# Weight halves interleaved word by word, moving tiles read from the last word down

## The chip, the core and the metric

The kernel runs on one core of a Trainium2 chip. The metric is the device time of one execution in microseconds (us). Five engines work side by side, each on its own queue of instructions: TensorE (PE in the profile; its weight loads are shown as PEld), VectorE (DVE), ScalarE (ACT), GpSimd (POOL) and SyncE (SP, which here only issues DMAs). Operands lie in SBUF, 128 partitions wide; matmul results lie in PSUM. An instruction that needs another engine's result waits on a semaphore.

A matmul has two operands. The stationary one (the weights, here 128 x 128) is loaded into the array by a weight load of its own; the moving one (here 128 x 256 or 128 x 512) is then streamed through. The weight load of the next matmul runs beside the streaming of the current one.

## The reference

One decoder layer on 512 tokens with a model width of 1024, all in float32:

```python
x = x + 0.5 * swiglu(rms_norm(x, g_ffn1), w_ffn1_gate, w_ffn1_up, w_ffn1_down)
proj = rms_norm(x, g_mix) @ w_in                 # 1024 x 1536
y_attn = sliding_window_attention(...)           # 8 heads, window 128, rotary, sinks
y_conv = conformer_conv(...)                     # 31 taps, LayerNorm, swish
y_mem  = memory_cross_attention(...)             # 4 heads, 256 memory tokens
x = x + concatenate([y_attn, y_conv, y_mem]) @ w_out
x = x + 0.5 * swiglu(rms_norm(x, g_ffn2), w_ffn2_gate, w_ffn2_up, w_ffn2_down)
```

with `swiglu(x, g, u, d) = (silu(x @ g) * (x @ u)) @ d` and a hidden width of 2816. Nearly all of the arithmetic is in the two SwiGLU blocks.

## The kernel before

**Precision by three products.** Every large product is made of float32r matmuls. Each operand is split into a high half (a copy cast to float32r) and a low half (the value less its high half). A product is then high x high, high x low and low x high, added up in PSUM. `mm3` (L339) issues these three for each block of 128 rows of the contraction: L347 and L348 both take the high weights `wh`, with the high and the low moving tile; L349 takes the low weights `wl` with the high moving tile. `product` (L439) does the same in L444 to L446.

**Weights.** The class `Weights` (L86) is a queue. Each item is a tile of 128 x 1024 float32 that a DMA brings from memory (`load_to`, L132), three loads ahead. `split_to` (L145) runs three items ahead of use: ScalarE writes the high half (L167), VectorE the low half (L168). The two halves are two tiles of 1056 words, `whi` and `wlo`, in four slots each; the half starts in its tile at a distance that `off` chooses (L159 to L162). With a tile of 4224 bytes both halves of an item begin at the same distance past a multiple of 256 bytes: 0 where `off` is 0, 128 where it is 128. A third kind of item, `vhi` and `vlo` (512 columns, L154), comes from the weights of the up product. The first two items are split in pieces by hand (`load_piece`, `split_piece`, L174 to L180), so that the first matmuls can start early.

**Moving tiles.** The activations' halves are tiles of 128 x 512 from `atile` (L291): `xh`, `xl` (the scaled input), `hh`, `hl` (the hidden layer), `yh`, `yl` (the outputs of the three head groups, some of them from the pool `mix`, L757) and `mh`, `ml` (the memory tokens). ScalarE writes the high one, VectorE the low one (for example L358 and L359, L402 and L403). Two small tiles named `shift` (L287, L430) only move what is allocated behind them by 128 and 64 bytes.

**The feed-forward blocks.** `ffn` (L394) runs over 22 blocks of 128 hidden columns. The first four are direct: gate and up, 8 x 3 matmuls with 512 moving columns each. From the fifth on, `fast` (L448) makes gate and up of a block together as a 2 x 2 block product in Strassen's way, with seven products of 256 moving columns (7 x 4 x 3 matmuls) in place of eight. Their moving tiles `bh` and `bl` (L427) are made once by `blocks`; the sums of weights that they need come from `make_sums` (L120). The down product runs in six rounds (`ROUNDS`, L77) between these blocks (`down`, L484). In the first round its matmuls have 512 moving columns, later on two times 256.

**The middle.** `mixing` (L747) projects the input (`proj`, 12 weight items, 512 moving columns) and runs convolution, windowed attention and memory attention in an order written out by hand (`ORDER`, L65). The attention products, transposes and sums are plain float32 matmuls (for example L826, L877, L948, L962). The output product goes through `mm3` again. The memory tokens are projected inside the first feed-forward block (`memory`, L580); for the values (L646 to L648) the roles are swapped, so that `mh` and `ml` are the weights of TensorE and the weight tile is the moving one.

Of the kernel before, what the change touches and what calls it, by code (L numbers as in the profile page):

```python
# [31 lines left out]
F32R = mybir.dt.float32r  # L32
# [6 lines left out]
P = 128  # L39
T = 512  # L40
KT = 8
# [37 lines left out]
N_ACT = 20  # L79
# [6 lines left out]
class Weights:  # L86
# [5 lines left out]
    def __init__(self, nc, pool, dma_ahead, conv_ahead, bufs):  # L92
        self.nc, self.pool = nc, pool
        self.dma_ahead, self.conv_ahead, self.bufs = dma_ahead, conv_ahead, bufs
        self.loads, self.items = [], []
        self.raw, self.after, self.split, self.piece = {}, {}, {}, {}
        self.sums = {}
        self.extra = None
        self.by_hand = 2
        self.loaded = self.done = self.at = self.turn = 0  # L100

    def add(self, ap, off=0):

        self.loads.append(ap)
        i = len(self.loads) - 1
        self.items.append((i, int(np.prod(ap.shape[1:])), off, lambda: self.raw[i]))

    def add_pair(self, gate, up, mid):
# [36 lines left out]
    def split_to(self, n):  # L145
        nc = self.nc
        while self.done < min(n, len(self.items)):
            i = self.done
            need, cols, off, src = self.items[i]
            self.load_to(need + 1)  # L150
            if need in self.after:
                self.after.pop(need)()
            if off is None:
                hi, lo = (self.extra.tile([P, cols], F32R, tag=t, name=f"{t}{i}", bufs=1) for t in ("vhi", "vlo"))  # L154
            else:

                j = self.turn % self.bufs[1]
                self.turn += 1
                hi, lo = (  # L159
                    self.pool.tile([P, 1024 + 32], F32R, tag=f"{t}{j}", name=f"{t}{i}", bufs=1)[:, c : c + 1024]  # L160
                    for t, c in (("whi", off // 4), ("wlo", 32 - off // 4))
                )  # L162
            if i < self.by_hand:
                self.piece[i] = (src(), hi, lo)
            else:
                raw = src()
                nc.scalar.copy(hi[:, :cols], raw[:, :cols])  # L167
                nc.vector.tensor_tensor(lo[:, :cols], raw[:, :cols], hi[:, :cols].bitcast(F32), op=ALU.subtract)  # L168
            self.split[i] = (hi, lo)
            self.done += 1  # L170
            if i >= self.by_hand:
                self.load_to(need + 1 + self.dma_ahead)
# [16 lines left out]
def per_load(r):  # L189

    return 8 // (ROUNDS[r][1] - ROUNDS[r][0])


def steps(f):

    r = next(r for r, (lo, hi) in enumerate(ROUNDS) if lo <= f < hi)
    if r == 0:
        return [], [], []
    m = KT // per_load(0)
    if r == 1:  # L200
        i = f - ROUNDS[1][0]
        return [(0, g) for g in range(m - 1)] if i == 0 else [], [(0, m - 1)] if i == 1 else [], []

    queue = [(q, g) for q in range(1, len(ROUNDS) - 1) for g in range(KT // per_load(q))]
    return [], [queue[f - ROUNDS[2][0]]], []


def layer(tc, ctx, a):
# [10 lines left out]
    def nm(s):  # L219
        uid[0] += 1  # L220
        return f"{s}_{uid[0]}"
# [10 lines left out]
    def work():  # L232
        return tmp.tile([P, T], F32, tag="t", name=nm("t"), bufs=5)
# [5 lines left out]
    W = Weights(nc, wpool, dma_ahead=3, conv_ahead=3, bufs=(4, 4))  # L239

    def flat(w):
        return w.rearrange("p k m -> p (k m)")

    def ffn_weights(n, memory):
        gu = a[f"wgu{n}"]

        def down(r, g):
            lo, hi = ROUNDS[r]
            m = per_load(r)
            return a[f"wd{n}"][g * m : (g + 1) * m, :, lo:hi].rearrange("d p k m -> p d (k m)")  # L250

        for f in range(NF):
            pre, mid, post = steps(f)
            for d in pre:
                W.add(down(*d), 128)
            if f < N_DIRECT:
                W.add(flat(gu[f, 0]))
                W.add(flat(gu[f, 1]))
            else:
                W.add_pair(flat(gu[f, 0]), flat(gu[f, 1]), [down(*d) for d in mid])  # L260
            for d in post:
                W.add(down(*d), 128)
            if memory and f == MEM_F:
                for t in range(2):
                    W.add(flat(a["wmk"][t]), 128)
                for c in range(2):
                    W.add(flat(a["wmv"][:, 4 * c : 4 * c + 4]))
        r = len(ROUNDS) - 1
        for g in range(KT // per_load(r)):
            W.add(down(r, g), 128)  # L270

    ffn_weights(1, True)
    for t in range(12):
        W.add(flat(a["win"][t]))
# [4 lines left out]
    for d in range(6, KT):  # L279
        W.add(flat(a["wout_z"][d - 6]))  # L280
    ffn_weights(2, False)


# [4 lines left out]
    act = ctx.enter_context(tc.tile_pool(name="act", bufs=1))  # L288
    xh, xl = {}, {}

    def atile(name, dtype=F32R):  # L291
        return act.tile([P, T], dtype, tag="h", name=nm(name), bufs=N_ACT)

    nc.scalar.dma_start(par, a["par"])
    warm = tmp.tile([P, T], BF16, tag="t", name="warm", bufs=5)
# [98 lines left out]
    def ffn(pool, norm, first, gain, hooks, next_gain, last):  # L394
# [3 lines left out]
        bh, bl = {}, {}  # L398
# [18 lines left out]
        def blocks(k):  # L417

            raw = pool.tile([P, 4, 256], F32, tag="sum", name=nm("braw"), bufs=SUM_BUFS)
            made = pool.tile([P, 4, 256], F32, tag="sum", name=nm("bmade"), bufs=SUM_BUFS)  # L420
            flat_raw = raw.rearrange("p a b -> p (a b)")
            for i, d in enumerate((k + 4, k)):
                DVE.scalar_tensor_tensor(
                    flat_raw[:, i * T : (i + 1) * T], x[:, d], par[:, gain + d : gain + d + 1], rb, op0=ALU.mult, op1=ALU.mult
                )
            b21, b22, b11, b12 = (raw[:, i] for i in range(4))
            bh[k] = pool.tile([P, 7, 256], F32R, tag="bh", name=nm("bh"), bufs=4)  # L427
            bl[k] = pool.tile([P, 7, 256], F32R, tag="bl", name=nm("bl"), bufs=4)
            if k == 0:
                pool.tile([P, 16], F32, name=nm("shift"))  # L430
            ACT.copy(bh[k][:, 4:7], raw[:, 0:3])
            DVE.tensor_tensor(made[:, B_T3 : B_Q1 + 1], raw[:, 1:3], raw[:, 3:4].to_broadcast([P, 2, 256]), op=ALU.subtract)
            DVE.scalar_tensor_tensor(made[:, B_Q2], made[:, B_T3], -1.0, b11, op0=ALU.mult, op1=ALU.subtract)
            DVE.tensor_tensor(made[:, B_T4], b21, made[:, B_Q2], op=ALU.add)
            ACT.copy(bh[k][:, 0:4], made)
            DVE.tensor_tensor(bl[k][:, 4:7], raw[:, 0:3], bh[k][:, 4:7].bitcast(F32), op=ALU.subtract)
            DVE.tensor_tensor(bl[k][:, 0:4], made, bh[k][:, 0:4].bitcast(F32), op=ALU.subtract)
# [142 lines left out]
    def memory():  # L580
# [7 lines left out]
        def piece(c):  # L588
                mh, ml = st.setdefault("mh", []), st.setdefault("ml", [])
                raw = st["raw", c]  # L590
                hi, lo = atile("mh"), atile("ml")
                sq = work()
                r0 = 0
                ACT.activation(sq, raw[:, r0 : r0 + T], AF.Square)
                for j in range(2):
                    k = 2 * c + j
                    g = par[:, C_GMEM + k : C_GMEM + k + 1]
                    r = raw[:, r0 + j * ML : r0 + (j + 1) * ML]
                    s = slice(j * ML, (j + 1) * ML)
                    ACT.activation(hi[:, s], r, AF.Identity, scale=g)  # L600
                    DVE.scalar_tensor_tensor(lo[:, s], r, g, hi[:, s].bitcast(F32), op0=ALU.mult, op1=ALU.subtract)
                mh.append(hi)
                ml.append(lo)
                if c == 0:
                    st["tot"] = tmp.tile([P, T], F32, tag="sqsum", name="mtot", bufs=1)
                    ACT.copy(st["tot"], sq)
                else:
                    POOL.dma_start(st["tot"], sq, accum_op=ALU.add)
# [65 lines left out]
        def part2():  # L674
# [5 lines left out]
            DVE.tensor_tensor(m, m, ps, op=ALU.mult)  # L680

        return load, piece, sums, part1, part2


# [62 lines left out]
def mixing(tc, nc, a, mix, W, norm, e):  # L747
# [4 lines left out]
    mm3, xhk, xlk, rsqrt, nm = (e[n] for n in ("mm3", "xhk", "xlk", "rsqrt", "nm"))  # L752
    scaled_split, Norm = e["scaled_split"], e["Norm"]

    atile = e["atile"]
    spare = (N_ACT - 2 * KT) // 2
    yh = [atile("yh") if k < spare else mix.tile([P, T], F32R, name=f"yh{k}") for k in range(KT)]  # L757
    yl = [atile("yl") if k < spare else mix.tile([P, T], F32R, name=f"yl{k}") for k in range(KT)]
    pad = mix.tile([P, 2, T + 32], F32, name="pad")
    conv = mix.tile([P, 2, T], F32, name="conv")  # L760
    kT = mix.tile([P, T], F32, name="kT")
# [235 lines left out]
    v = {}  # L997
# [237 lines left out]
```

## Time and profile before

| | |
|---|---|
| median of 3 runs | 864.93 us |
| lowest and highest | 864.52 and 865.8 us |
| span of the profiled execution (first to last instruction) | 862.3 us |
| granted TensorE clock, mean over the span | 1.000 |
| DMA, mean over the span | 106 GB/s |

The profiled execution is another one than the three that were timed; its span leaves out what lies before the first and after the last instruction. Times in the timeline count from the span's start. A row of a group names the line, the engine, the operation, what it writes and reads (output <- inputs), the shapes and the count; behind the first bar stand busy time in us and the mean of one in ns, behind the second the idle time before it and what ended it. A row of the timeline has start and duration in us. A row of the windows has, after the stretch and its length, for PE, PEld, DVE, ACT and POOL the busy time and the number of instructions, and then the granted clock, the share of the DMA engines and GB/s; with one line of the program chosen, only that line's engine is shown.

### The profile page before, as it was taken

How to read it: one execution, taken by the hardware profiler on the slowest of the kernel's cores; microseconds unless marked ns; L12 is line 12 of the kernel's file. 1: busy time of each engine (PE TensorE's matmuls, PEld its weight loads, DVE VectorE, ACT ScalarE, POOL GpSimd, SP SyncE). 2: the span in 40 equal slices, each digit the busy share in tenths (PEclk: the TensorE clock that was granted, in tenths of full speed). 3: DMA queues.
4: the chain of work that ended last, by engine and by line, in shares of the span. 5: the costliest groups of instructions: out<-in, count | busy, mean ns of one | idle time of the engine just before them, and what ended most of it. 6: DMA issues, size and time to landing. Idle time of an engine off the chain costs nothing.

```text
span 862.3 us, 15722 instructions
## 1 busy us (share of the span) xinstructions
PE 855.5 (99%) x6361; PEld 789.7 (92%) x6361; DVE 697.0 (81%) x1163; ACT 446.1 (52%) x741; POOL 27.4 (3%) x30
## 2 busy tenths in 40 slices
PE   9999999999999999999999999999999999999998
PEld 5889999999999999988776888889999999999998
DVE  7998877877868897869989985997887868787772
ACT  7455555455654444533948763454654544544540
POOL 0000000000000000300000030010000000000000
PEclk9999999999999999999999999999999999999999
DMA  7326333334553334222010423335333343323312
GB/s 273 123 78 168 97 100 122 100 112 133 142 143 120 123 110 130 74 98 62 5 57 14 133 75 103 94 91 154 99 98 123 98 122 97 109 92 100 120 49 99
DMA packets 34809, 91.45 MB, mean 106 GB/s; under 512 B 3248, under 2 KB 5808, under 8 KB 34736
## 3 DMA queue, kind: packets, MB, share of 16 engines
q1 hardware_dynamic: 32000, 85.99, 32.1%
q0 software_dynamic: 1584, 2.88, 2.1%
q10 hardware_dynamic: 1152, 1.57, 0.6%
q8 instruction: 50, 0.82, 0.4%
q14 instruction: 23, 0.19, 0.1%
HBM read 85.45 MB, written 2.10 MB: 102 GB/s over the span
## 4 chain that ended last, share of the span: by engine, by line
PE 92%; DVE 3%; ACT 2%; issue 1%; DMA 1%; SPq 0%; ACTq 0%; DVEq 0%
PE mm L347 14%; PE mm L349 14%; PE mm L348 14%; PE mm L444 11%; PE mm L445 11%; PE mm L446 11%; PE sc L444 2%; PE sc L445 2%; PE sc L446 2%; PE sc L349 1%; PE sc L347 1%; PE sc L348 1%; PE tp L948 1%; PE tp L962 1%; ACT p L913 1%
## 5 line engine op out<-in xcount | busy, mean ns | idle before, releaser
L444 PE MATMUL mm<-bh,whi 128*128 128x256 f32 x864 | 238.8, 276 | 0.2 <-ACT kept L459 0.2
L445 PE MATMUL mm<-bl,whi 128*128 128x256 f32 x864 | 238.5, 276 | 0.0
L446 PE MATMUL mm<-bh,wlo 128*128 128x256 f32 x864 | 238.5, 276 | 0.0
L348 PE MATMUL mm<-hl,whi 128*128 128x256 f32 (+1 forms) x640 | 183.9, 288 | 0.0
L349 PE MATMUL mm<-hh,wlo 128*128 128x256 f32 (+1 forms) x640 | 183.9, 288 | 0.0
L347 PE MATMUL mm<-hh,whi 128*128 128x256 f32 (+1 forms) x640 | 183.3, 288 | 0.0
L167 ACT CAST whi<-wraw 128x1024 fp32r<-128x1024 f32 (+2 forms) x122 | 124.2, 1021 | 102.5 <-PE mm L348 37.9
L168 DVE TENSOR_TENSOR wlo<-wraw,whi 128x1024 fp32r<-128x1024 f32 (+2 forms) x122 | 144.5, 1187 | 27.9 <-ACT whi L167 27.3
L444 PEld LDWEIGHTS mm<-bh,whi 128*128 128x128 f32 x864 | 162.2, 188 | 0.6 <-ACT kept L459 0.4
L445 PEld LDWEIGHTS mm<-bl,whi 128*128 128x128 f32 x864 | 162.2, 188 | 0.2
L446 PEld LDWEIGHTS mm<-bh,wlo 128*128 128x128 f32 x864 | 162.2, 188 | 0.0
L349 PEld LDWEIGHTS mm<-hh,wlo 128*128 128x128 f32 x640 | 120.2, 188 | 2.9
L347 PEld LDWEIGHTS mm<-hh,whi 128*128 128x128 f32 x640 | 120.2, 188 | 2.7
L348 PEld LDWEIGHTS mm<-hl,whi 128*128 128x128 f32 x640 | 120.2, 188 | 2.7
L168 DVE TENSOR_TENSOR wlo<-s,whi 128x1024 fp32r<-128x1024 f32 x72 | 87.9, 1222 | 34.7 <-ACT whi L167 34.4
L167 ACT CAST whi<-s 128x1024 fp32r<-128x1024 f32 x72 | 75.5, 1051 | 46.1 <-PE mm L445 42.3
L347 PE MATMUL mm<-xh,whi 128*128 128x512 f32 x192 | 76.6, 403 | 0.3 <-ACT whi L179 0.3
L348 PE MATMUL mm<-xl,whi 128*128 128x512 f32 x192 | 75.6, 394 | 0.6 <-DVE xl L359 0.5
L349 PE MATMUL mm<-xh,wlo 128*128 128x512 f32 x192 | 75.9, 395 | 0.0
L506 DVE SCALAR_TENSOR_TENSOR x<-mm,x 128x512 f32<-128x512 f32 x80 | 54.0, 682 | 3.3 <-PE mm L349 3.3
L167 ACT CAST vhi<-wraw 128x512 fp32r<-128x512 f32 x36 | 22.4, 622 | 60.9 <-PE sc L445 46.8
L126 DVE TENSOR_TENSOR s<-wraw 128x512 f32<-128x512 f32 x36 | 24.9, 691 | 33.5 <-DMA wraw<-in_wgu 33.5
(244 smaller groups left out, 1368.2 us busy)
## 6 DMA issues: line engine op xcount, KB each, us to landing
wraw<-in_wgu SPq DMA_DIRECT2D x86, 512.0 KB, 3.6
wraw<-in_wd SPq DMA_DIRECT2D x44, 512.0 KB, 3.6
wraw<-in_win SPq DMA_DIRECT2D x12, 512.0 KB, 3.5
x<-t POOLq DMA_DIRECT2D x8, 256.0 KB, 6.1
out<-t SPq DMA_DIRECT2D x7, 256.0 KB, 2.0
x<-in_xT SPq DMA_DIRECT2D x3, 512.0 KB, 6.8
wraw<-in_wout_a SPq DMA_DIRECT2D x6, 256.0 KB, 2.9
wraw<-in_wgu SPq DMA_DIRECT2D x4, 256.0 KB, 5.4
```

The source lines that it names most:

```text
L126: nc.vector.tensor_tensor(s12[:, l], u[:, l], u[:, r], op=ALU.add)
L167: nc.scalar.copy(hi[:, :cols], raw[:, :cols])
L168: nc.vector.tensor_tensor(lo[:, :cols], raw[:, :cols], hi[:, :cols].bitcast(F32), op=ALU.subtract)
L347: PE.matmul(ps[:, t], wh[:, w], hi(k)[:, t], start=one, stop=False, skip_group_check=cut > 1)
L348: PE.matmul(ps[:, t], wh[:, w], lo(k)[:, t], start=False, stop=False, skip_group_check=cut > 1)
L349: PE.matmul(ps[:, t], wl[:, w], hi(k)[:, t], start=False, stop=end, skip_group_check=cut > 1)
L444: PE.matmul(ps, wh[:, c], bh[k][:, block], start=one, stop=False, skip_group_check=not first)
L445: PE.matmul(ps, wh[:, c], bl[k][:, block], start=False, stop=False, skip_group_check=not first)
L446: PE.matmul(ps, wl[:, c], bh[k][:, block], start=False, stop=end, skip_group_check=not first)
L506: DVE.scalar_tensor_tensor(o, ps, 0.5, xd, op0=ALU.mult, op1=ALU.add)
L913: ACT.activation(self.p[n, h][:, c], src[h][:, i, c], AF.Exp, scale=self.fac[:, m : m + 1], bias=self.neg[:, m : m + 1], accum_out=self.de ...
L948: PE.transpose(ps[:, i * P : (i + 1) * P], self.p[n, h][:, c : c + P], ident)
```

## The change

The high and the low half of a weight item share one tile, `both`. The high half takes the even words and the low half the odd words. An item that is marked `straight` (the memory's value weights, which are the moving operand) keeps the two halves one behind the other. All moving tiles (`atile`, `bh`, `bl`, and those of `yh`, `yl` in the pool `mix`) are seen through a reversed view: column 0 lies at the last word of the tile. `mh` and `ml` are reversed twice, so they lie as before. The argument `off` still says which items are of the third kind, and its value no longer moves anything.

```diff
-    def add(self, ap, off=0):
+    def add(self, ap, off=0, straight=False):
         self.loads.append(ap)
         i = len(self.loads) - 1
+        if straight:
+            self.straight.add(len(self.items))
...
             if off is None:
-                hi, lo = (self.extra.tile([P, cols], F32R, tag=t, name=f"{t}{i}", bufs=1) for t in ("vhi", "vlo"))
+                both = self.extra.tile([P, 2 * cols + 16], F32R, tag="v", name=f"v{i}", bufs=1)[:, 16:]
+                hi, lo = both[:, 0::2], both[:, 1::2]
             else:
                 j = self.turn % self.bufs[1]
                 self.turn += 1
-                hi, lo = (
-                    self.pool.tile([P, 1024 + 32], F32R, tag=f"{t}{j}", name=f"{t}{i}", bufs=1)[:, c : c + 1024]
-                    for t, c in (("whi", off // 4), ("wlo", 32 - off // 4))
-                )
+                both = self.pool.tile([P, 2048 + 64], F32R, tag=f"w{j}", name=f"w{i}", bufs=1)[:, 48 : 48 + 2048]
+                if i in self.straight:
+                    hi, lo = both[:, :1024], both[:, 1024:]
+                else:
+                    hi, lo = both[:, 0::2], both[:, 1::2]
...
-                    W.add(flat(a["wmv"][:, 4 * c : 4 * c + 4]))
+                    W.add(flat(a["wmv"][:, 4 * c : 4 * c + 4]), 0, True)
...
     def atile(name, dtype=F32R):
-        return act.tile([P, T], dtype, tag="h", name=nm(name), bufs=N_ACT)
+        return act.tile([P, T], dtype, tag="h", name=nm(name), bufs=N_ACT)[:, ::-1]
...
-            bh[k] = pool.tile([P, 7, 256], F32R, tag="bh", name=nm("bh"), bufs=4)
-            bl[k] = pool.tile([P, 7, 256], F32R, tag="bl", name=nm("bl"), bufs=4)
+            bh[k] = pool.tile([P, 7, 256], F32R, tag="bh", name=nm("bh"), bufs=4)[:, :, ::-1]
+            bl[k] = pool.tile([P, 7, 256], F32R, tag="bl", name=nm("bl"), bufs=4)[:, :, ::-1]
...
-                hi, lo = atile("mh"), atile("ml")
+                hi, lo = atile("mh")[:, ::-1], atile("ml")[:, ::-1]
...
-    yh = [atile("yh") if k < spare else mix.tile([P, T], F32R, name=f"yh{k}") for k in range(KT)]
-    yl = [atile("yl") if k < spare else mix.tile([P, T], F32R, name=f"yl{k}") for k in range(KT)]
+    yh = [atile("yh") if k < spare else mix.tile([P, T], F32R, name=f"yh{k}")[:, ::-1] for k in range(KT)]
+    yl = [atile("yl") if k < spare else mix.tile([P, T], F32R, name=f"yl{k}")[:, ::-1] for k in range(KT)]
```

More of the change, by code (lines that the diff above doesn't have):

```diff
@@ L97, in __init__ @@
         self.sums = {}
+        self.straight = set()
         self.extra = None
```

## The prediction

> **What bounds the kernel now.** I read the page from its busy line to its chain, then the windows of the stages, and last the timeline row by row, because a page cannot tell how densely matmuls follow each other.
>
> ```profile
> span 862.3 us, 15722 instructions
> PE 855.5 (99%) x6361; PEld 789.7 (92%) x6361; DVE 697.0 (81%) x1163; ACT 446.1 (52%) x741; POOL 27.4 (3%) x30
> PEclk9999999999999999999999999999999999999999
> PE 92%; DVE 3%; ACT 2%; issue 1%; DMA 1%; SPq 0%; ACTq 0%; DVEq 0%
> ```
>
> TensorE is busy from end to end at the full granted clock, and 92% of the chain that ended last is matmuls. So the time is the number of matmuls times the distance between their starts (the pitch), plus little. The duration in a row is not that distance, since matmuls overlap. The pitch has to be read from starts. The groups of the program's large products:
>
> ```profile
> L444 PE MATMUL mm<-bh,whi 128*128 128x256 f32 x864 | 238.8, 276 | 0.2 <-ACT kept L459 0.2
> L347 PE MATMUL mm<-hh,whi 128*128 128x256 f32 x576 | 159.0, 276 | 0.0
> L444 PE MATMUL sc<-bh,vhi 128*128 128x256 f32 x144 | 39.8, 276 | 0.0
> L347 PE MATMUL mm<-xh,whi 128*128 128x512 f32 x192 | 76.6, 403 | 0.3 <-ACT whi L179 0.3
> L347 PE MATMUL mm<-hh,whi 128*128 128x512 f32 x64 | 24.3, 395 | 0.0
> L347 PE MATMUL mm<-yh,whi 128*128 128x512 f32 x48 | 18.6, 405 | 1.1 <-DVE s L895 1.0
> L347 PE MATMUL sc<-xh,whi 128*128 128x512 f32 x32 | 12.6, 394 | 0.0
> L347 PE MATMUL sc<-yh,whi 128*128 128x512 f32 x16 | 6.1, 394 | 0.0
> ```
>
> Each of these lines has two sisters (high times low, low times high) with the same count. That makes 3 x (864 + 576 + 144) = 4752 matmuls with 256 moving columns. With 512 columns there are 3 x (192 + 48 + 32 + 16) = 864 whose weights start at offset 0 and 3 x 64 = 192 whose weights start at offset 128. The timeline gives their pitches; in each fence the first and the last row of an unbroken run are shown.
>
> ```profile
> 302.06 0.28 PE L444 MATMUL sc<-bh,vhi 128*128 128x256 f32 x1
> ...
> 306.14 0.28 PE L347 MATMUL mm<-hh,whi 128*128 128x256 f32 x1
> ...
> 397.57 0.39 PE L349 MATMUL mm<-xh,wlo 128*128 128x512 f32 x1
> ...
> 401.01 0.40 PE L349 MATMUL mm<-xh,wlo 128*128 128x512 f32 x1
> ...
> 62.73 0.40 PE L349 MATMUL mm<-hh,wlo 128*128 128x512 f32 x1
> ...
> 66.47 0.40 PE L348 MATMUL mm<-hl,whi 128*128 128x512 f32 x1
> ...
> 265.31 0.28 PE L349 MATMUL mm<-mh,wlo 128*128 128x256 f32 x1
> ...
> 266.49 0.28 PE L347 MATMUL mm<-mh,whi 128*128 128x256 f32 x1
> ```
>
> There are 36 pitches in the first run (4.08/36 = 113.3 ns), 15 in the second (3.44/15 = 229.3 ns), 16 in the third (3.74/16 = 233.8 ns) and 10 in the fourth (1.18/10 = 118.0 ns). The first and the fourth do the same work on tiles of the same size and shape and differ only in which tiles; so do the second and the third. So a matmul of one shape has more than one speed here, at the same clock and with nothing waited for. The weights of the next matmul are loaded beside the current one, so the suspect is that two reads of SBUF hinder each other depending on where they stand.
>
> How fast could it be? Two rows bound it. Where the moving operand has two columns, only the weight load is left:
>
> ```profile
> 403.26 0.97 PEld L826 LDWEIGHTS tp<-pair,t 128*128 128x128 f32 x8 [0.33 <-issue]
> 404.15 0.19 PEld L347 LDWEIGHTS mm<-xh,whi 128*128 128x128 f32 x1
> 418.62 0.87 PE tp L948 x8
> ```
>
> Eight loads take 404.15 - 403.26 = 0.89 us, 111.3 ns each. The last row, from the chain, is eight transposes of 128 columns: 108.75 ns for a load and a pass, the densest pairs of that kind in the trace.
>
> **The change part by part.** No instruction is added or removed. Four things move.
>
> (1) The weights' high and low halves lie word by word in one tile, so a weight column is 8 bytes from the next instead of 4. (2) The moving tiles are written and read from their last word down. By the program's allocation a moving slot starts 64 bytes past a multiple of 256, so its reading now starts at 60 past one (64 + 2044) and goes down. Weight tiles start 192 past; the last column of a block of 128 is at 192 + 1016, which is 184 past for high and 188 for low. If a load takes its last column first, both reads go down, 124 or 128 bytes apart. 128 columns of 8 bytes are the 1024 bytes that 256 moving columns of 4 bytes cover, and the two rows above say both last about as long (111.3 and 113.3 ns), so the distance holds. No row shows the direction of a load; that is an assumption.
>
> What would it be worth? If no read hinders the other, 256 columns cannot go below the load: 111.3 ns, a gain of 2.0 ns x 4752 = 9.5 us. For 512 columns I take twice that, 222.6: 6.7 ns x 864 = 5.8 us and 11.2 ns x 192 = 2.2 us. The sum is 17.5 us; 92% of the chain is matmuls, so 16.1 us. The other end, by the transposes (108.75 and 217.5 ns): 4.55 x 4752 + 11.8 x 864 + 16.3 x 192 = 34.9 us, of which 92% is 32.1 us. On the bad side the two streams may settle where the fourth stretch stands, 118.0 ns, and 236 for 512 columns: 4.7 x 4752 + 6.7 x 864 + 2.2 x 192 = 28.5 us, 26.2 us of it on the path. I take the first end because its row is the load of the very same 128 x 128 words; the transposes' loads are another kind (140 ns a row instead of 188).
>
> [...]
>
> (3) ScalarE and VectorE write every other word of the weight tile (L167, L168), VectorE also reads it so, and the moving halves are written backwards.
>
> ```profile
> L167 ACT CAST whi<-wraw 128x1024 fp32r<-128x1024 f32 (+2 forms) x122 | 124.2, 1021 | 102.5 <-PE mm L348 37.9 <-issue 30.4 <-PE mm L445 22.6
> L168 DVE TENSOR_TENSOR wlo<-wraw,whi 128x1024 fp32r<-128x1024 f32 (+2 forms) x122 | 144.5, 1187 | 27.9 <-ACT whi L167 27.3
> L359 DVE SCALAR_TENSOR_TENSOR xl<-x,par,xh x24: 735/752/1798, 4.9 to 525.9; 128x512 fp32r<-128x512 f32 x24
> ```
>
> The number of words stays, so I cost the new order at nothing. No row has a strided write of this size. The bounds are 0 and a doubling; the only stretched VectorE instruction in the trace is the slowest of L359, 1798 against a median of 752. What covers a longer split is VectorE's idle time, and it is thin in places. First VectorE's stages, then L168's part of them:
>
> ```profile
> 40.00:100.00 60.00, 60.00 (x369) 53.19 (x368) 55.56 (x76) 31.03 (x44) 3.63 (x4) 1.00 0.44 120
> 100.00:340.00 240.00, 239.82 (x2114) 239.62 (x2113) 191.35 (x281) 122.26 (x189) 2.76 (x5) 1.00 0.40 121
> 535.00:600.00 65.00, 65.00 (x357) 55.92 (x356) 59.30 (x92) 32.51 (x44) 3.47 (x4) 1.00 0.41 112
> 600.00:800.00 200.00, 200.00 (x1741) 198.92 (x1741) 158.03 (x205) 100.51 (x154) 0.00 (x0) 1.00 0.36 107
> ...
> 40.00:100.00 60.00, 20.02 (x18) 1.00 0.44 120
> 100.00:340.00 240.00, 89.15 (x81) 1.00 0.40 121
> 535.00:600.00 65.00, 18.74 (x17) 1.00 0.41 112
> 600.00:800.00 200.00, 76.53 (x69) 1.00 0.36 107
> ```
>
> In the third number pair VectorE has 55.56 of 60 us, and L168 20.02 of these: 4.44/20.02, a split 22% longer fills it. In the two long stages it takes 48.65/89.15 and 41.97/76.53, 55%.
>
> [...]
>
> (4) The two halves share one tile. Where the order of work is kept by whole tiles, TensorE waits for the low half before it uses the high one, and the next write of a slot waits for the last reader of both, one matmul (0.11 us) later. In the steady loops the split is three items ahead, which hides it. At the start nothing does:
>
> ```profile
> 5.96 0.69 DVE L180 TENSOR_TENSOR wlo<-wraw,whi 128x512 fp32r<-128x512 f32 x1 [0.28 <-ACT whi L179]
> 5.98 0.80 PE L347 MATMUL mm<-xh,whi 128*128 128x512 f32 x1
> ```
>
> The first matmul starts beside the low split, so up to 0.7 us is lost; I count 0.7.
>
> The sum is -16.1 + 0.7 = -15.4 us, a span of 846.9 us. The median of the runs shown, 864.93, is 2.6 us above the profiled span; with the same 2.6 it is **849.5 us**. Measurements of this kernel can tell about 0.2% (1.7 us) from no change.
>
> **The rivals.**
>
> *The reads don't hinder each other (no change).* Then 113.3 and 229.3 ns are the array's own pitch and the time is 862.3 + 0.7 + 2.6, about 865 us. For it: the lowest pitches of 256 and 512 columns are nearly 1 to 2, as a rate of the array would be. Against it: 118.0 and 233.8 for the same shapes.
>
> *The streams run in step, but at the wrong distance (slower).* A fixed distance is also one that never gets better. If the load runs upwards, or starts some 13 ns earlier or later than assumed (128 bytes at 1024 bytes in 111 ns), the distance may be a colliding one all along. The price is the 118.0 ns of the fourth stretch: 862.3 + 26.2 + 0.7 + 2.6 = 892 us. For it: the stretch with 118.0 ns holds its pitch over ten matmuls, so such a state is stable.
>
> *VectorE becomes the bound (slower).* It decides from a split 22% longer. Doubled splits overrun the four stages above by 15.6, 40.5, 13.0 and 34.6 us: 969 us. Against it: only the cover is thin, no row shows the slowdown.
>
> *TensorE itself reads strided or downward words at half rate (slower).* A load of 223 ns instead of 111 would bind every 256-column matmul: 110 x 4752 = 523 us more, about 1390 us. No row has such a read.
>
> **How the numbers follow.** Forecast, streams that no longer collide, wholly or in part: 0.59, between 833 us (by the transposes: 862.3 - 32.1 + 2.6) and 862 us. No change: 0.11. Wrong distance: 0.12, up to 892. VectorE: 0.10. Half rate: 0.08. The range 833 to 892 leaves out the last two, 0.18. Faster 0.59, same 0.11, slower 0.30.
>
> **What would show it.** Right: runs as at 302 us with starts 111 to 112 ns apart, 512 columns at 223 or less, L167 and L168 still at 1021 and 1187 ns, weight loads still 188 ns a row. Wrong distance: pitches near 118 and 236 with L168 unchanged. VectorE: L168 over 1450 ns, TensorE waiting for wlo. Half rate: the weight loads' rows longer, or the pitch near 223. The forecast fails above all if a load does not read from its last column down.

## The result and the profile after

| | before | after |
|---|---|---|
| median of 4 runs | 864.72 us | 889.32 us |
| lowest and highest | 863.56 and 865.8 us | 888.65 and 890.19 us |
| span of the profiled execution | 862.3 us | 886.8 us |

The ratio is 1.0282, with a 95% interval of 1.0263 to 1.0302: the changed kernel is slower by 24.6 us. Lines of the changed program stand five further down than before: L347 to L349 are now L352 to L354, L444 to L446 are L449 to L451, L167 and L168 are L172 and L173. First the head, the clock and the chain from the page of the changed kernel.

```profile
span 886.8 us, 15629 instructions
PE 879.4 (99%) x6361; PEld 817.1 (92%) x6361; DVE 699.7 (79%) x1163; ACT 471.0 (53%) x741; POOL 27.1 (3%) x30
PEclk9999999999999999999999999999999999999999
PE 95%; ACT 2%; DVE 2%; DMA 1%; issue 0%; SPq 0%; ACTq 0%; DVEq 0%
```

TensorE still has 6361 matmuls at the full granted clock, is still busy 99% of the span, and its share of the chain has grown. Nothing new stands between the matmuls; they have become slower themselves. The timeline of TensorE shows by how much. As in the prediction, the first and the last row of unbroken runs are given, and the difference of their starts divided by the number of steps is the pitch.

```profile
302.00 0.28 PE L449 MATMUL mm<-bh,w 128*128 128x256 f32 x1
...
307.65 0.28 PE L449 MATMUL mm<-bh,w 128*128 128x256 f32 x1
...
408.10 0.40 PE L354 MATMUL mm<-xh,w 128*128 128x512 f32 x1
...
409.97 0.40 PE L353 MATMUL mm<-xl,w 128*128 128x512 f32 x1
...
62.39 0.40 PE L354 MATMUL mm<-hh,w 128*128 128x512 f32 x1
...
67.99 0.40 PE L354 MATMUL mm<-hh,w 128*128 128x512 f32 x1
```

With 256 columns there are 48 steps in 5.65 us, 117.7 ns each (113.3 before). With 512 columns there are 8 steps in 1.87 us, 233.8 ns (229.3 before), and 24 steps in 5.60 us, 233.3 ns (233.8 before). Over all such matmuls the trace has means of 117.8 and about 233.4 ns. So 4.5 ns x 4752 = 21.4 us, 4.1 ns x 864 = 3.5 us, and -0.4 ns x 192 = -0.1 us: 24.8 us, against 24.5 us by which the span has grown. The whole loss is matmul pitch, and 86% of it belongs to the matmuls with 256 columns.

Three groups of the changed kernel tell more (line, engine, operation, names, shapes and count, then busy us and mean ns, then idle time before): the weight load of the largest product and the two splits.

```profile
L449 PEld LDWEIGHTS mm<-bh,w 128*128 128x128 f32 x864 | 169.3, 196 | 0.2
...
L172 ACT CAST w<-wraw 128x1024 fp32r<-128x1024 f32 (+2 forms) x122 | 137.9, 1133 | 99.7 <-PE mm L354 37.2
...
L173 DVE TENSOR_TENSOR w<-wraw,w 128x1024 fp32r<-128x1024 f32 (+2 forms) x122 | 145.2, 1190 | 44.6 <-ACT w L172 43.2
```

The same load in the kernel before, from the same view:

```profile
L444 PEld LDWEIGHTS mm<-bh,whi 128*128 128x128 f32 x864 | 162.2, 188 | 0.6 <-ACT kept L459 0.4
```

A load takes 196 ns in its row instead of 188. VectorE's split is where it was (1190 against 1187 ns), ScalarE's is 11% longer (1133 against 1021), but ScalarE has nearly 100 us of idle time ahead of it in this group.

### The profile page after: what moved, and what is told of

Same layout as the page of the kernel before. It is cut to its first block, busy times and chain, and to the rows that moved or that the text cites. A ratio compares the mean times of both kernels' runs of the same rounds, so it can differ in the third digit from the quotient of the medians.

```text
span 886.8 us, 15629 instructions
## 1 busy us (share of the span) xinstructions
PE 879.4 (99%) x6361; PEld 817.1 (92%) x6361; DVE 699.7 (79%) x1163; ACT 471.0 (53%) x741; POOL 27.1 (3%) x30
## 4 chain that ended last, share of the span: by engine, by line
PE 95%; ACT 2%; DVE 2%; DMA 1%; issue 0%; SPq 0%; ACTq 0%; DVEq 0%
PE mm L352 15%; PE mm L354 15%; PE mm L353 15%; PE mm L449 12%; PE mm L451 11%; PE mm L450 11%; PE sc L449 2%; PE sc L451 2%; PE sc L450 2%; PE sc L354 1%; PE sc L353 1%; PE sc L352 1%; PE tp L953 1%; ACT p L918 1%; PE tp L967 1%; DMA wraw<-in_wgu 1%
## 5 line engine op out<-in xcount | busy, mean ns | idle before, releaser
L449 PE MATMUL mm<-bh,w 128*128 128x256 f32 x864 | 243.8, 282 | 0.0
L451 PE MATMUL mm<-bh,w 128*128 128x256 f32 x864 | 243.6, 282 | 0.0
L450 PE MATMUL mm<-bl,w 128*128 128x256 f32 x864 | 243.6, 282 | 0.0
L172 ACT CAST w<-wraw 128x1024 fp32r<-128x1024 f32 (+2 forms) x122 | 137.9, 1133 | 99.7 <-PE mm L354 37.2
L354 PE MATMUL mm<-hh,w 128*128 128x256 f32 (+1 forms) x640 | 187.5, 294 | 0.0
L353 PE MATMUL mm<-hl,w 128*128 128x256 f32 (+1 forms) x640 | 187.5, 294 | 0.0
L352 PE MATMUL mm<-hh,w 128*128 128x256 f32 (+1 forms) x640 | 187.0, 294 | 0.0
L173 DVE TENSOR_TENSOR w<-wraw,w 128x1024 fp32r<-128x1024 f32 (+2 forms) x122 | 145.2, 1190 | 44.6 <-ACT w L172 43.2
L449 PEld LDWEIGHTS mm<-bh,w 128*128 128x128 f32 x864 | 169.3, 196 | 0.2
L450 PEld LDWEIGHTS mm<-bl,w 128*128 128x128 f32 x864 | 169.3, 196 | 0.2
L451 PEld LDWEIGHTS mm<-bh,w 128*128 128x128 f32 x864 | 168.6, 195 | 0.0
L352 PEld LDWEIGHTS mm<-hh,w 128*128 128x128 f32 x640 | 125.2, 196 | 2.4
L354 PEld LDWEIGHTS mm<-hh,w 128*128 128x128 f32 x640 | 124.8, 195 | 2.6
L173 DVE TENSOR_TENSOR w<-s,w 128x1024 fp32r<-128x1024 f32 x72 | 88.1, 1223 | 46.6 <-ACT w L172 46.4
L172 ACT CAST w<-s 128x1024 fp32r<-128x1024 f32 x72 | 84.2, 1169 | 22.9 <-PE mm L451 18.9
L352 PE MATMUL mm<-xh,w 128*128 128x512 f32 x192 | 77.0, 405 | 1.1 <-ACT w L184 1.1
L354 PE MATMUL mm<-xh,w 128*128 128x512 f32 x192 | 76.5, 399 | 0.0
L352 PEld LDWEIGHTS mm<-xh,w 128*128 128x128 f32 x192 | 37.2, 194 | 10.9 <-ACT w L184 2.0
```

The costliest lines, as they stand in the source:

```text
L352: PE.matmul(ps[:, t], wh[:, w], hi(k)[:, t], start=one, stop=False, skip_group_check=cut > 1)
L353: PE.matmul(ps[:, t], wh[:, w], lo(k)[:, t], start=False, stop=False, skip_group_check=cut > 1)
L354: PE.matmul(ps[:, t], wl[:, w], hi(k)[:, t], start=False, stop=end, skip_group_check=cut > 1)
L449: PE.matmul(ps, wh[:, c], bh[k][:, block], start=one, stop=False, skip_group_check=not first)
L450: PE.matmul(ps, wh[:, c], bl[k][:, block], start=False, stop=False, skip_group_check=not first)
L451: PE.matmul(ps, wl[:, c], bh[k][:, block], start=False, stop=end, skip_group_check=not first)
```

## The experiments

Three theories are named by letters in the expectations. **A**: a load of every other word takes longer by itself, and the load is what binds a matmul of 256 columns. **B**: the two streams do run in step, but at a distance at which they collide all the time. **C**: reading the moving operand downwards costs something by itself. "Distance" is the start of the weights less the start of the moving tile, modulo 256 bytes; in the kernel before it is 64 for the matmuls with 256 columns, in the changed one 128. That places a multiple of 256 bytes apart are alike is the author's assumption. It fits the trace of the kernel before, where the two halves of an item lie so by the program: the steps from L445 to L446 (the low half is loaded meanwhile) and from L446 to L444 (a high half) both have a mean of 113.3 ns.

### One half of the change alone

The first kernel interleaves the weights and reads the moving tiles upwards as before:

```diff
-                hi, lo = (
...
-                    for t, c in (("whi", off // 4), ("wlo", 32 - off // 4))
-                )
+                both = self.pool.tile([P, 2048 + 64], F32R, tag=f"w{j}", name=f"w{i}", bufs=1)[:, 48 : 48 + 2048]
...
+                    hi, lo = both[:, 0::2], both[:, 1::2]
```

> Only the interleaving of the weight halves is kept; all moving tiles lie and are read upwards as in the kernel before. Three theories of the 24.6 us. A, the load of every other word takes longer by itself (its rows went from 188 to 196 ns) and binds a matmul of 256 columns: about 889 us, 256 columns at 117 to 118 ns, loads at 196 ns a row. B, the two streams go in step at a colliding distance: without the common direction they slide past each other, so the time leaves 889, to 865 or below, and the pitch leaves 117.8 ns. C, reading the moving tile downwards costs the 4.5 ns: about 865 us, 113.3 ns, loads at 188 ns.

The second keeps the weights as before and turns the moving tiles round:

```diff
-        return act.tile([P, T], dtype, tag="h", name=nm(name), bufs=N_ACT)
+        return act.tile([P, T], dtype, tag="h", name=nm(name), bufs=N_ACT)[:, ::-1]
...
-            bh[k] = pool.tile([P, 7, 256], F32R, tag="bh", name=nm("bh"), bufs=4)
+            bh[k] = pool.tile([P, 7, 256], F32R, tag="bh", name=nm("bh"), bufs=4)[:, :, ::-1]
```

> Only the downward moving tiles are kept; the weight halves lie in two tiles of their own as in the kernel before. A (the load of every other word is longer): about 865 us, 113.3 ns, loads at 188 ns a row. B (in step at a colliding distance): the streams are not in step here, 860 to 870 us. C (downward reading costs): about 889 us, 117.8 ns with loads at 188 ns.

Interleaving alone gave 903.87 us, a ratio of 1.0433 (1.0394 to 1.0472). The timeline of that kernel, first and last row of an unbroken run:

```profile
301.82 0.29 PE L449 MATMUL mm<-bh,w 128*128 128x256 f32 x1
...
306.07 0.28 PE L354 MATMUL mm<-hh,w 128*128 128x256 f32 x1
```

That is 35 steps in 4.25 us, 121.4 ns. None of the three theories had forecast a time above 889 us here. Turning alone gave 888.76 us, 1.0266 (1.0234 to 1.0298). Its weight loads, from the view by groups, and two runs of its timeline:

```profile
L444 PEld LDWEIGHTS mm<-bh,whi 128*128 128x128 f32 x864 | 162.4, 188 | 0.2
```

```profile
243.65 0.28 PE L444 MATMUL mm<-bh,whi 128*128 128x256 f32 x1
...
247.77 0.28 PE L446 MATMUL mm<-bh,wlo 128*128 128x256 f32 x1
...
301.88 0.28 PE L444 MATMUL mm<-bh,whi 128*128 128x256 f32 x1
...
306.92 0.28 PE L444 MATMUL mm<-bh,whi 128*128 128x256 f32 x1
```

35 steps in 4.12 us are 117.7 ns; 42 steps in 5.04 us, in the same execution, are 120.0 ns. The loads are the old ones at 188 ns, and yet the kernel is as slow as the changed one. So turning the moving tiles is enough for the whole loss, with no interleaving at all. Interleaving is not innocent either: alone it costs more than both parts together. With the weights interleaved, turning the tiles as well does help (117.8 ns instead of 121.4), but from a worse place than the kernel before.

### Another distance

If the distance of 128 were the culprit (B), moving the weights by half of 256 bytes should help:

```diff
-                both = self.pool.tile([P, 2048 + 64], F32R, tag=f"w{j}", name=f"w{i}", bufs=1)[:, 48 : 48 + 2048]
+                both = self.pool.tile([P, 2048 + 64], F32R, tag=f"w{j}", name=f"w{i}", bufs=1)[:, 16 : 16 + 2048]
```

> The changed kernel with all weight tiles moved by 128 bytes against the moving tiles (16 words into the tile instead of 48, 48 instead of 16 for the third kind). A: the distance doesn't matter, 889 us within 2 us, 117.8 ns. B: 128 bytes is half of the period of 256, so this is the opposite place; if 889 us is the colliding one, the pitch falls to 111 to 113 ns and the time to 850 to 865 us. C: 889 us.

It gave 902.06 us, 1.0416 (1.0384 to 1.0449), with a pitch of 120.0 ns, 51 steps in 6.12 us of its timeline:

```profile
305.85 0.28 PE L450 MATMUL mm<-bl,w 128*128 128x256 f32 x1
...
311.97 0.28 PE L450 MATMUL mm<-bl,w 128*128 128x256 f32 x1
```

The distance of the change is thus the better of the two, and again no theory had forecast the time (889 us by A and C, 850 to 865 by B). To see more distances, bare matmuls were put ahead of the kernel before, so that this run's total time (1263.1 us) means nothing. Each section repeats one matmul 24 times (12 times with 512 columns):

```diff
+        for cols, n in ((256, 24), (512, 12)):
+            for step in (1, 2):
+                for d, m in (("u", up), ("d", down)):
+                    for s in range(16):
+                        run(f"{'xy'[step - 1]}{d}{'hf'[cols // 512]}{LET[s]}", n, step, m, 4 * s, cols)
```

The names say x for weights word by word and y for every other word, u or d for moving up or down, h for 256 and f for 512 columns, and a letter for the distance in steps of 16 bytes (a is 0, e 64, i 128).

> The kernel before with a run of bare matmuls on constant tiles ahead of it, so its time is about 865 us and that run, some 350 us, together; only the pitches of the run are read. It has weight loads nearly alone (2 moving columns) from every word, every other word and every fourth word, and then matmuls of 256 and of 512 columns for weights at step 1 and 2, moving up and down, at 16 distances 16 bytes apart. A: loads alone 111.7 ns at step 1 and 115 to 118 at step 2; 256 columns at step 2 near 117.8 at all 16 distances and in both directions. B: loads alone the same at step 1 and 2; at step 2 downwards some distances at 111 to 113 ns and others at 118 or more, with the distance of the changed kernel (letter i) among the latter. C: downward runs 4 to 5 ns above upward ones at both steps.

Each row of the timeline is a whole section. Its length less the last matmul (0.28 us), divided by 23, is the pitch:

```profile
44.44 2.89 PE L227 MATMUL xuhe<-mv,wt 128*128 128x256 f32 x24
...
89.86 2.99 PE L227 MATMUL xdhe<-mv,wt 128*128 128x256 f32 x24
...
147.02 3.06 PE L227 MATMUL yuhi<-mv,wt 128*128 128x256 f32 x24
...
170.07 3.04 PE L227 MATMUL ydha<-mv,wt 128*128 128x256 f32 x24
172.95 2.99 PE L227 MATMUL ydhb<-mv,wt 128*128 128x256 f32 x24
...
192.74 2.99 PE L227 MATMUL ydhi<-mv,wt 128*128 128x256 f32 x24
...
209.71 3.04 PE L227 MATMUL ydho<-mv,wt 128*128 128x256 f32 x24
...
257.25 2.90 PE L227 MATMUL xufp<-mv,wt 128*128 128x512 f32 x12
```

| section | set as in | pitch in the section | pitch in that kernel | its time |
|---|---|---|---|---|
| xuhe | before | 113.5 ns | 113.3 ns | 864.7 us |
| xdhe | tiles turned only | 117.8 ns | 117.7 to 120.0 ns | 888.8 us |
| ydhi | the change | 117.8 ns | 117.7 ns | 889.3 us |
| ydha | weights moved 128 bytes | 120.0 ns | 120.0 ns | 902.1 us |
| yuhi | interleaved only | 120.9 ns | 121.4 ns | 903.9 us |

Two operand streams alone give the pitch of each of these five kernels, within 0.5 ns where it is a single one; in the last run of this kind the windows show no busy time of VectorE, ScalarE and GpSimd beside them (0.00 us from 100 to 150 us). From ydhb to ydho, 13 distances in a row, 312 steps take 36.76 us, 117.8 ns: with both parts of the change, the distance hardly matters, as it intends. But none of the 16 is below that. Slower places, as B has them, stand only at the edges (120 to 121 ns at a, o and p).

The sections also show what A and C got wrong. Both expected one shift for all distances: A 117.8 ns wherever the weights are interleaved, C 4 to 5 ns more wherever the tiles are read downwards. Read upwards, interleaved weights take 117.8 ns at one distance only (yuhf) and up to 122 at the others. And with weights in a row, the average over the distances is nearly the same upwards (118.1 ns, xuhb to xuhp) and downwards (118.6 ns, xdha to xdhp). What upward reading has and downward reading lacks is a good place: xuhe, the distance of the kernel before, is 3 ns below the next best.

### Where the floor lies

The next two runs of this kind take the streams apart: loads with hardly a stream, streams with thin weights (32 columns, whose load has a row of 110 ns beside 256 moving columns instead of 188; the quarter in the expectation is the author's estimate), other widths, and 64 distances of 4 bytes.

```diff
+        for cols, c in ((512, "f"), (384, "t"), (256, "h")):
+            for d, m in (("u", up), ("d", down), ("s", two)):
+                run("thin" + d + c, 16, 1, m, 0, cols, 32)
...
+        for d, m in (("u", up), ("d", down)):
+            for step, x in ((1, "p"), (2, "pp")):
+                for cols, c in ((128, "q"), (192, "o"), (224, "n"), (256, "h"), (320, "k"), (384, "t"), (512, "f")):
+                    run(f"width{x}{d}{c}", 16, step, m, 16 if d == "u" else 32, cols)
```

> The kernel before with another run of bare matmuls ahead of it; only the pitches of that run are read. First loads nearly alone at every word, every other and every third. Then thin weights (32 columns, so the load is a quarter as long) with 512, 384 and 256 moving columns read up, down and at every other word upwards: if downward reading has a cost of its own, the difference of 512 and 256 columns is larger downwards (about 116 ns for 256 columns against about 107 to 113 upwards); if the 233.3 ns of downward runs came from the load beside it, up and down are alike. Then all 64 distances in steps of 4 bytes for weights at step 1 and upward reading: if the distance decides, 256 columns reach 113.3 ns only near 64 bytes and 512 columns reach 226.7 only near 16 and 240. Last, 7 widths of 128 to 512 columns at steps 1 and 2, up and down: where the load binds, the pitch stays at the load's 111.7 (step 1) or 117.8 ns (step 2) for the narrow widths and rises only when the stream becomes the longer one.

For narrow streams the width hardly shows in the pitch, so it is taken to be the load's. In the timeline of this run, p is for words in a row and pp for every other word, q for 128 and h for 256 columns; thinsh reads every other word of the moving tile:

```profile
62.83 3.83 PE L228 MATMUL thinsh<-mv,wt 128*32 128x256 f32 x16
66.48 1.86 PE L228 MATMUL finehaa<-mv,wt 128*128 128x256 f32 x14
...
93.00 1.76 PE L228 MATMUL finehea<-mv,wt 128*128 128x256 f32 x14
...
338.91 1.90 PE L228 MATMUL widthpdq<-mv,wt 128*128 128x128 f32 x16
...
344.26 2.09 PE L228 MATMUL widthpdh<-mv,wt 128*128 128x256 f32 x16
...
355.10 1.99 PE L228 MATMUL widthppdq<-mv,wt 128*128 128x128 f32 x16
...
362.63 2.51 PE L228 MATMUL widthppdk<-mv,wt 128*128 128x320 f32 x16
```

From widthpdq to widthpdh, 48 matmuls of 128 to 224 columns take 5.35 us, 111.5 ns each: the load of words in a row (111.3 in the prediction's row of loads, with two moving columns). From widthppdq to widthppdk, 64 matmuls of 128 to 256 columns take 7.53 us, 117.7 ns each: the load of every other word, 6 ns longer, with a downward stream of any of these widths beside it (119.1 ns with an upward one, at the one distance tried). This is the longer load of theory A, shown. It also means that about 117.8 ns is the floor of 256 columns once the weights are interleaved, and neither direction went below it at any distance tried; the change reaches that floor. Of the 32 distances upwards from 0 to 124 bytes (finehaa to finehhd, words in a row) finehea, the kernel before's own, is the lowest: (1.76 - 0.28)/13 = 113.8 by its row. The next has 114.6 (finehfc), the others 115 to 122; finehaa, for one, has (1.86 - 0.28)/13 = 121.5. From 128 to 240 bytes the steps of 16 bytes in the first run of bare matmuls (xuhi to xuhp) have 116.5 or more. With 512 columns and 216 to 252 bytes (finefnc to finefpd) the lowest have 227.5 ns by their rows, at 240, where it was expected, and at 252; the others have 231 to 234.

The last run of this kind does the same for the direction:

```diff
+        for s in range(16):
+            run("evenload" + LET[s], 12, 2, up, 4 * s, 2)
...
+        for d, m in (("u", up), ("d", down)):
+            for cols, c, n in ((256, "h", 14), (512, "f", 9)):
+                for s in range(16):
+                    run(f"thin{d}{c}{LET[s]}", n, 1, m, 4 * s, cols, 32)
+        for cols, c, n in ((256, "h", 14), (512, "f", 9)):
+            for s in range(64):
+                run(f"downfine{c}{LET[s // 4]}{LET[s % 4]}", n, 1, down, s, cols)
```

> The kernel before with a third run of bare matmuls ahead; only their pitches are read. Loads nearly alone at every other word, at 16 distances: 117.8 ns at all of them if the load itself is longer, 111.7 at some if the 117.8 was a matter of place. Thin weights (32 columns) upwards and downwards at 16 distances, 256 and 512 columns: if a downward stream is slower by itself, 117.7 and 233.3 ns at all of them and 113.3 and 226.7 upwards at many. Downward with full weights at step 1 at all 64 distances: no 113.3 ns anywhere if downward reading rules that pitch out; some if it was only the 16 distances tried.

Its timeline; here the pitch is the difference of two starts divided by the matmuls between them:

```profile
21.69 1.55 PE L228 MATMUL evenloadb<-mv,wt 128*128 128x2 f32 x12
...
24.52 2.05 PE L228 MATMUL evenloadd<-mv,wt 128*128 128x2 f32 x12
...
69.01 1.81 PE L228 MATMUL thinuha<-mv,wt 128*32 128x256 f32 x14
...
81.97 1.75 PE L228 MATMUL thinuhi<-mv,wt 128*32 128x256 f32 x14
...
85.15 1.80 PE L228 MATMUL thinuhk<-mv,wt 128*32 128x256 f32 x14
...
94.83 2.24 PE L228 MATMUL thinufa<-mv,wt 128*32 128x512 f32 x9
...
143.07 1.81 PE L228 MATMUL thindhj<-mv,wt 128*32 128x256 f32 x14
...
151.31 1.81 PE L228 MATMUL thindho<-mv,wt 128*32 128x256 f32 x14
...
154.62 2.27 PE L228 MATMUL thindfa<-mv,wt 128*32 128x512 f32 x9
...
186.13 2.26 PE L228 MATMUL thindfp<-mv,wt 128*32 128x512 f32 x9
188.23 1.82 PE L228 MATMUL downfinehaa<-mv,wt 128*128 128x256 f32 x14
...
294.81 2.27 PE L228 MATMUL downfinefaa<-mv,wt 128*128 128x512 f32 x9
```

Loads of every other word alone: 24 in 2.83 us, 117.9 ns. Only the first three of the 16 distances could be read at the full clock (last section), so that the place plays no part in it is shown for these alone.

With thin weights, an upward stream of 256 columns takes 113.6 ns where it is quick (thinuhi and thinuhj, 28 matmuls in 3.18 us). It is that quick, within a nanosecond, at half of the 16 distances; at the others it takes up to 117.9, and 115.3 on average (224 from thinuha to thinufa in 25.82 us). A downward one takes 117.7 ns where it is quickest (70 from thindhj to thindho in 8.24 us) and 118.2 on average. Downwards with 512 columns it is 233.4 ns at all 16 distances together (135 in 31.51 us); upwards it is 231.4 on average and 228.2 at best, and the 226.7 expected at many distances did not come.

With full weights, the 64 downward distances from downfinehaa on take 119.0 ns on average (896 in 106.58 us), and none is below 117.5. So theory C is shown as a floor, though not as a shift of every pitch: at the distances tried, a downward stream of 256 columns has a floor of about 117.7 ns and one of 512 of about 233.4, even where the weights have a quarter of their columns, and no good place below it. Why it has none is not shown. The change imposes both floors, A's and C's, and they happen to be the same 117.7 ns; so taking back either half alone could not bring the old pitch back.

### Can the kernel before be improved instead?

In the first run of bare matmuls, 512 columns upwards reached about 228 ns at a distance of 240 (xufp above, 2.90 us less 0.39 over 11; the 226.7 of the expectation below is what 16 bytes, xufb, gave). The kernel before has 192 (229.3 ns) and, in the first round of down products, 64 (233.8 ns). One kernel gives all matmuls with 512 columns the distance 240 and leaves those with 256 columns at 64; a second leaves the first round at 64; a third only puts both halves into one tile, one behind the other, at the old distances. The cut of the first two is shown; in the third, `c` is `off // 4`.

```diff
-                hi, lo = (
...
-                    for t, c in (("whi", off // 4), ("wlo", 32 - off // 4))
-                )
+                both = self.pool.tile([P, 2048 + 64], F32R, tag=f"w{j}", name=f"w{i}", bufs=1)
+                c = (off or 48) // 4
+                hi, lo = both[:, c : c + 1024], both[:, c + 1024 : c + 2048]
```

> The kernel before, with the weights of all 512-column matmuls 240 bytes past the moving tile, modulo 256, where the bare run had 226.7 ns, instead of 192 (229.3 ns) and 64 (233.8 ns); the 256-column ones stay at 64 bytes. Both halves share one tile, one behind the other. If the distance of the two reads sets the pitch in the kernel as in the bare run: 864 x 2.6 + 192 x 7.1 ns = 3.6 us less, about 861.5 us, with 226 to 227 ns for the three lines. If the kernel's pitches depend on more than that: no change, or up to 2 us more for the shared tile.

> As e6, but the 192 matmuls of the first down round keep their weights at 64 bytes past the moving tile, so that the first block products are entered from the same matmuls as in the kernel before. In e6 the 256-column matmuls went to 117.8 ns at an unchanged distance. If the pipe has two lasting states at that distance and the way into it decides: 113.3 ns in both feed-forward blocks and 864 x 2.6 ns = 2.2 us less than before, about 863 us. If the shared tile causes the 117.8 ns: about 881 us again.

> The kernel before with both halves of an item in one tile, one behind the other, all distances modulo 256 as before. If the shared tile causes the 117.8 ns of e6: about 880 us. If two lasting states and the way into them do: 113.3 ns and 865 us, unless the slightly different waits at the start send it into the other state, and then stretches at 113.3 and at 117.8 ns in one and the same run, with no pitch between.

The first gave 881.72 us, 1.0185 (1.0161 to 1.021). Its timeline:

```profile
403.66 0.39 PE L346 MATMUL mm<-xh,w 128*128 128x512 f32 x1
...
407.51 0.39 PE L348 MATMUL mm<-xh,w 128*128 128x512 f32 x1
...
239.80 0.28 PE L445 MATMUL mm<-bh,w 128*128 128x256 f32 x1
...
246.16 0.28 PE L445 MATMUL mm<-bh,w 128*128 128x256 f32 x1
...
299.73 0.28 PE L445 MATMUL mm<-bh,w 128*128 128x256 f32 x1
...
305.51 0.28 PE L445 MATMUL mm<-bh,w 128*128 128x256 f32 x1
```

The 512 columns did as hoped: 17 steps in 3.85 us, 226.5 ns. But the 256 columns, at the distance they had before, ran at 117.8 ns (54 steps in 6.36 us) at 240 us and at 113.3 ns (51 in 5.78 us) at 300 us. An estimate from the times: 881.72 us are 16.4 more than the 865.27 of the kernel before beside it, though the 512 columns gain some 3.8 (2.8 ns x 864 and 7.3 x 192), and 20.2 us at 4.5 ns are about 4500 of the 4752 at the longer pitch. The second kernel took from 867.28 to 882.53 us over 12 executions (median 875.46; the seven quickest together 1.0057, 1.0027 to 1.0086), so neither of its two forecasts, 863 and 881 us, covers it. Its profiled execution, of 868.95 us, ran the 256 columns at 113.3 ns at 240 us (54 steps in 6.12 us) and at 117.7 at 320 us (52 steps in 6.12 us). That the executions of 882 us spent longer at the longer pitch fits their time, but none of them was profiled. The third gave 865.28 us, 0.9997 (0.9978 to 1.0015): one tile for both halves costs nothing. None of the three was faster than the kernel before.

## Why the prediction was wrong, step by step

**What bounds the kernel** held. The time is the count of matmuls times their pitch, and the change in pitch accounts for the change in time to 0.3 us.

**The step that failed** is "If no read hinders the other, 256 columns cannot go below the load: 111.3 ns", and with it the 222.6 ns for 512 columns. Of the old load it holds (111.5 ns with 128 to 224 columns, and no 256 columns below 113.3), and I used it as the value that the changed reads would take. Two things were wrong with that. The 111.3 ns is the load of words in a row; the load that the change makes takes 117.7 ns (widthppdq to widthppdk). And a stream of 256 columns has a floor of its own that is not the load: 113.3 ns upwards (113.6 with thin weights), 117.7 downwards. The matmuls with 256 columns were thus at the lowest pitch found already, at one of the few distances that have it, and a gain of 2.0 ns x 4752 was not to be had. Those with 512 columns had some room (229.3 against 226.5 ns at the distance 240), but not down to 222.6. In place of -9.5 us stands +21.4 us, in place of -5.8 us for the 864 matmuls with 512 columns +3.5 us, and in place of -2.2 us for the other 192 -0.1 us. The factor of 92% was not borne out either: the change of pitch summed over all these matmuls is 24.8 us, and the span grew by 24.5.

**The fourth stretch was misread.** I took 118.0 ns for a collision and 113.3 ns for a milder one. The runs show no lower pitch than 113.3 ns for that stream. Nor do the two stretches stand differently: by the program both have the distance 64 (the memory's key weights have `off` 128 and `mh` comes from `atile`, just as the down product's weights and `hh` in the first stretch). So the pair was no evidence that the place decides. It looks like the two lasting pitches of the last section, already in the kernel before. The observation that one shape has two speeds was right; that a third, lower one lies below them was a hope. The row that could have warned was there: 36 steps at 113.3 ns without a break are as steady as a floor.

**The rivals.** "In step, but at the wrong distance" was priced at 892 us by 118.0 ns, and 889.3 came out. That the two numbers are close is luck, and 889.3 lies inside the range only because this rival sets its upper end. The rival's mechanism is not what happened: 13 of 16 distances give the same 117.8 ns, and the other distance tried in the kernel was slower. "TensorE itself reads strided or downward words at half rate" had the right place, TensorE's own reads, and the wrong size: the load is 6% longer (117.7 against 111.5 ns), not 100%, and the floor of a downward stream of 256 columns 4% higher (117.7 against 113.3). Between no cost and a doubling I had no row, and put the chance at 0.08; a small cost in that place should have been the rival. "No change" fell with the pitch. "VectorE becomes the bound" did not occur.

**The writes (part 3)** cost VectorE nothing, as forecast: 1190 against 1187 ns. ScalarE's 11% (1133 against 1021 ns) was not foreseen, but stays covered.

TensorE's own reads are not as free: with every other word the load went from 111.5 to 117.7 ns, and a moving operand of 256 columns read so (thinsh) takes 3.65 us / 16 = 228 ns instead of 113.

**The shared tile (part 4)** costs nothing in the end (0.9997), and the wait of up to 0.7 us at the start did not appear. In the timeline of the changed kernel the first matmul still begins beside the low split:

```profile
6.25 0.69 DVE L185 TENSOR_TENSOR w<-wraw,w 128x512 fp32r<-128x512 f32 x1 [0.31 <-ACT w L184]
...
6.27 0.51 PE L352 MATMUL mm<-xh,w 128*128 128x512 f32 x1 [0.63 <-ACT w L184]
```

**The direction of a load**, named as the weakest assumption, is not needed to explain the loss: the floors of the longer load and of the downward stream do that. With the moving tiles turned, interleaved weights have one pitch, 117.8 ns, at 13 of 16 distances, which fits a load that takes its last column first; it isn't proved by it, and a load's own direction wasn't varied.

## What to carry to other kernels

Before a floor is borrowed from one row for another kind of access, measure the new access by itself: loads alone, streams with thin weights, a few dozen matmuls each. A pitch that holds over dozens of matmuls without a wait may be a floor rather than a collision, and then putting the streams in step has nothing to win. Here weights belong in adjacent words: loading every other word cost 6% of a load (117.7 against 111.5 ns). Rising order of the moving columns pays where the distance is a good one, 4% of a pitch of 256 columns (113.3 against 117.7 ns); averaged over the distances it made hardly a difference (118.1 against 118.6 ns). The kernel before had its tiles at such a distance, and the change gave that up.

## What the runs showed that was not expected

**Two lasting pitches at one distance.** The same matmuls at the same distance run at 113.3 ns in the kernel before, and most of them (the estimate above) at 117.8 ns in the one with the distance 240, both at a granted clock of 1.00. In the kernel with the distance 240 the pitch changes within one execution (fence above), and in the profiled execution of its sibling too. In the kernel with the tiles turned alone it changes between 117.7 and 120.0 ns. Upwards with full weights, 113 ns was reached at only one of the 32 distances from 0 to 124 bytes in the bare matmuls (113.8, finehea), and 114.6 at a second; downwards at none of 64 (117.5 or more). What decides which of the two is entered stays open. So a distance alone does not settle a pitch. It does move it: in the first run of bare matmuls, from 113.5 ns (xuhe) to 120.0 ns at other distances (xuhh, xuhi, xuhk, xuhp).

**The clock fell while only loads ran.** In the last run of bare matmuls, the windows of the chip's engines over the loads alone show it (after the stretch, PE, PEld, DVE, ACT and POOL busy with counts, then the granted clock):

```profile
21.00:24.00 3.00, 3.00 (x28) 3.00 (x27) 0.00 (x0) 0.00 (x0) 0.00 (x0) 1.00 0.02 5
27.00:57.00 30.00, 30.00 (x142) 30.00 (x142) 0.00 (x0) 0.00 (x0) 0.00 (x0) 0.50 0.00 1
```

TensorE is busy throughout, but with two moving columns a matmul the granted clock went from 1.00 to 0.50 about 5 us in. A load of every other word that took 117.9 ns before takes 213.3 ns after. Loads measured after that point can't be set beside the others.
